# Six buffers for spilled activations, expert rows three ahead, the first eight tiles' gates kept in SBUF, and stores on ScalarE's queue

## The chip, the cores and the metric

The kernel runs on one core of a Trainium2 chip. The metric is device time in microseconds (us) of one execution. Engines are called as the profile calls them: PE is TensorE's matrix multiply and PEld its weight load, DVE is VectorE, ACT is ScalarE, POOL is GpSimd, SP is SyncE, which issues most DMAs. SPq, POOLq and so on are the engines' queues of DMA issues and waits.

## The reference, cut to what matters

One decoder layer on 512 prompt tokens and 64 sample tokens: a gated short convolution and a sliding-window attention are merged, a layer norm follows, and then a mixer that picks experts by product keys. The mixer is where the change lies:

```python
def block_fn(xb):                       # tokens x 1024, 8 heads, 128 x 128 experts
    qv = jnp.einsum('nd,de->ne', xb, w_pq).reshape(PEER_BLOCK, PEER_HEADS, 2, D_HALF)
    s = jnp.einsum('nhpc,hpkc->nhpk', qv, sub_keys)
    top_s, top_i = lax.top_k(s, PEER_TOPK)                      # 16 of 128, per half
    cand_s = top_s[:, :, 0, :, None] + top_s[:, :, 1, None, :]
    best_s, sel = lax.top_k(cand_s.reshape(PEER_BLOCK, PEER_HEADS, -1), PEER_TOPK)
    ...
    gate = jax.nn.softmax(best_s, axis=-1)
    pre = jnp.einsum('nd,nhkd->nhk', xb, expert_u[idx])
    coef = gate * jax.nn.gelu(pre, approximate=False)
    return jnp.einsum('nhk,nhkd->nd', coef, expert_v[idx])
```

A second layer norm closes the layer.

## The kernel before, in words

Every product runs in three passes (`mm3`): each operand is split into a high part `whi` (copied by ACT, L119) and a remainder `wlo` (subtracted by POOL or DVE, L120). `table` loads a 512 KB weight block into `raw` (SP's queue, L138), splits it, and then lets `side` run some steps of side work.

The tokens are split in two. For 192 rows (`GATHER`) the chosen experts' rows are fetched one by one: `experts` issues one gather per step on POOL's queue (L512, 128 rows of 4 KB, 512 KB), and DVE folds a fetched row into a dot product (`junk`, L526) or into the output (`h`, L535). There are 384 such steps, and the tables `PACE_A`, `PACE_B`, `PACE_U` and `PACE_V` say how many are taken beside each weight block. The other 384 rows (`DENSE`) go through all 16384 experts, 128 at a time, in 128 tiles t:

- `front(t)`: 24 matmuls of 384 columns (L123 to L125) and a gelu on ACT. The first `NS` tiles are stored to DRAM (`spill`), the next `LAG` stay in SBUF (`gel`); so 69 fronts run ahead of the closing loop.
- `gate_matrix`: 24 groups of 16 tokens. DVE builds one-hot matrices (`hot`, L787, four per group), ACT and POOL scale them by the gates, PE multiplies them (L796), ACT and DVE copy the product to `gb`, and SP stores it to the DRAM tensor `gd` (L803). A scheduler that simulates the engines weaves the first 59 fronts around the scores and the groups; the ten fronts 59 to 68 are held behind the last group.
- the closing loop: `middle(t)` loads the gates of eight tiles at a time from `gd` into `gm` (L902) and the stored activation into `re` (L906), and multiplies them (L910); `back(t)` loads a block of `expert_v` (`raw<-in_ev`); 18 matmuls of 512 columns (L940) add the tile to six accumulators. Fronts 69 to 127 run in the second part of the same loop. The last two tiles' matmuls are L134.

`route` picks 16 of the candidates and turns their scores into gates (L447 to L452). `finish` is the closing layer norm (L190, L548 to L554), after which SP stores the output. The order of instructions on each engine is fixed when the kernel is built. Pools share SBUF by region: pool `v`, which holds `re`, `gm` and the `expert_v` blocks of later tiles, takes the place of pools that are closed before it.

Of the kernel before, what the change touches and what calls it, by code (L numbers as in the profile page):

```python
# [47 lines left out]
GN = 16  # L48
# [20 lines left out]
PACE_A, PACE_B, PACE_U, PACE_V = (1, 0), (2, 1, 1), (2, 1), (1, 3)  # L69
# [6 lines left out]
def step_kernel(ctx: ExitStack, tc: tile.TileContext, I: dict, O: dict):  # L76
# [86 lines left out]
    mask_p = const("mask_p", [128, 256], src=I["mask_p"])  # L163
# [9 lines left out]
    kT_all = const("kT_all", [128, SEQ])  # L173
    v_all = const("v_all", [128, 5, 128])
# [233 lines left out]
    def top16(val, pos, s, n):  # L408
        s2 = tmp("k", [128, 128], "s2", bufs=2)[:s.shape[0], :n]
        V.max(val[:, 0:8], s)  # L410
        V.max_index(pos[:, 0:8], val[:, 0:8], s)
        V.match_replace(s2, val[:, 0:8], s, -3.0e38)
        V.max(val[:, 8:16], s2)
        V.max_index(pos[:, 8:16], val[:, 8:16], s2)

    numbers, scratch = [iota], []

    def route(val, pos, sel, hs):

# [13 lines left out]
        def f128(tag, dt=F32):  # L433
# [15 lines left out]
        gs = scratch[0][:r, 128:132] if scratch else tmp("k", [128, 4], "gs")[:r]  # L449
        V.tensor_reduce(gs, ge, axis=AX.X, op=ALU.add)  # L450
        V.reciprocal(gs, gs)
        V.tensor_tensor(gt.rearrange("p (h k) -> p h k", h=4), ge,  # L452
                        gs.unsqueeze(2).broadcast_to([r, 4, 16]), op=ALU.mult)

        mk = f128("mk")
        V.tensor_single_scalar(mk, bp, 64, op=ALU.is_ge)
        pf = tmp("k", [128, 4, 2, 16], "pf", dt=BF16)[:r]
        V.tensor_copy(pf, pos.rearrange("p (h s) k -> p h s k", s=2))
        for k, (s1, s2, off) in enumerate((((4, ALU.logical_shift_right), (2, ALU.logical_shift_right), -12.0),
# [9 lines left out]
            oh = tmp("k", [128, 4, 16, 16], "oh", dt=BF16)[:r]  # L469
# [111 lines left out]
    def weight(s, src):  # L581
# [3 lines left out]
        if s.units > LO_N:  # L585
            return table(src, "w", G)
# [146 lines left out]
    def scores(s, g4):  # L733
# [21 lines left out]
        for i, r in enumerate(s.rows):  # L755
# [3 lines left out]
            sc = tmp("kb"[s.w], [128, 4, 128], "sc", bufs=2 + s.w * 2)  # L759
# [14 lines left out]
    def gate_matrix(i, keys, gt, gd):  # L774
# [6 lines left out]
        for g in range(128 // GN):  # L781
# [21 lines left out]
            S.dma_start(gd[i * (128 // GN) + g], gb)  # L803
# [48 lines left out]
    pools["b"] = bs.enter_context(pool("b", "right"))  # L852
# [3 lines left out]
    def front(t):  # L856
        wu = table(I["euT"][t], "w", G if t < AHEAD else V, PACE_U[t % len(PACE_U)] if t < AHEAD else 0)
# [194 lines left out]
```

## Time and profile before

| what | us |
|---|---|
| median of three runs (lowest, highest) | 1848.39 (1845.89, 1849.37) |
| the profiled execution, whole | 1850.18 |
| its span, first to last instruction | 1848.4 |
| PE busy | 1723.9 (93%) |
| PE weight loads busy | 1566.4 (85%) |
| DVE busy | 1464.7 (79%) |
| ACT busy | 781.4 (42%) |
| POOL busy | 1109.6 (60%) |

PE is busy 93% of the span, but its matmuls overlap and their ends are modelled, so the rate at which they start tells more than the busy time. The 124 us in which PE is idle are not spread evenly, and neither is the work of the DMA engines: the page's slices show 130 GB/s near the start and 300 to 350 GB/s in the second half. Each stage has to be read for itself.

### The profile page before, as it was taken

What the parts mean: (1) busy time and instruction counts of PE and PEld (TensorE: products, weight loads), DVE (VectorE), ACT (ScalarE), POOL (GpSimd) and SP (SyncE); (2) the same over time, 40 slices, a digit from 0 to 9 for tenths busy, and PEclk for the clock granted to TensorE, in tenths of its full rate; (3) what the DMA queues carried; (4) which work ended last, traced back from release to release, by engine and by line L of the source; (5) the groups of instructions that cost most, each with busy time, mean ns of one, the idle gap of its engine ahead of it and who ended that gap; (6) DMA issues with size and microseconds to landing.
All of it is one profiled execution on the core that took longest, in us unless ns stands there. A gap on an engine that the chain in (4) does not pass through costs nothing.

```text
span 1848.4 us, 27569 instructions
## 1 busy us (share of the span) xinstructions
PE 1723.9 (93%) x9760; PEld 1566.4 (85%) x9760; DVE 1464.7 (79%) x2588; ACT 781.4 (42%) x1337; POOL 1109.6 (60%) x724
## 2 busy tenths in 40 slices
PE   7999998998799999899888899999999999999985
PEld 7998898988489899799878778778999999999974
DVE  5634579998965699987893778779788878888887
ACT  4554444443233344377794333333333333343322
POOL 4445434367857777798645422224678787778783
PEclk9999999999989999899999999999999999999998
DMA  7446443368757789899748899999999999989873
GB/s 252 134 150 225 138 132 122 115 200 300 249 201 241 235 294 311 271 349 348 289 188 303 317 333 335 336 346 339 333 314 345 337 324 350 353 307 343 314 268 104
DMA packets 190539, 496.50 MB, mean 269 GB/s; under 512 B 17712, under 2 KB 83696, under 8 KB 187312
## 3 DMA queue, kind: packets, MB, share of 16 engines
q1 hardware_dynamic: 135104, 293.39, 46.5%
q0 software_dynamic: 55296, 201.35, 30.2%
q8 instruction: 76, 1.25, 0.3%
q14 instruction: 63, 0.52, 0.1%
HBM read 454.48 MB, written 40.54 MB: 268 GB/s over the span
## 4 chain that ended last, share of the span: by engine, by line
PE 40%; DVE 23%; DMA 14%; issue 9%; POOL 8%; ACT 4%; SPq 1%; DVEq 0%; POOLq 0%; ACTq 0%
PE acc L940 15%; PE ps L123 7%; PE ps L124 7%; PE ps L125 7%; DMA g<-in_ev,idx 5%; POOL wlo L120 4%; POOL g L512 4%; DVE junk L526 3%; PE ps L796 3%; DMA re<-spill 2%; DVE wlo L120 2%; DMA raw<-in_ev 2%; DMA raw<-in_w_o 1%; ACT whi L119 1%; ACT hot L793 1%
## 5 line engine op out<-in xcount | busy, mean ns | idle before, releaser
L120 POOL TENSOR_TENSOR wlo<-raw,whi 128x1024 fp32r<-128x1024 f32 x232 | 579.1, 2499 | 301.8 <-ACT whi L119 264.7
L119 ACT ACTIVATE whi<-raw 128x1024 fp32r<-128x1024 f32 x388 | 409.5, 1056 | 603.9 <-PE ps L124 236.1
L123 PE MATMUL ps<-xhi,whi 128*128 128x384 f32 (+2 forms) x1600 | 529.9, 331 | 21.6 <-ACT sp L863 13.4
L125 PE MATMUL ps<-xhi,wlo 128*128 128x384 f32 (+2 forms) x1600 | 526.1, 329 | 3.5 <-POOL wlo L120 2.0
L124 PE MATMUL ps<-xlo,whi 128*128 128x384 f32 (+2 forms) x1600 | 526.1, 329 | 0.0
L535 DVE SCALAR_TENSOR_TENSOR h<-g,pre,h 128x1024 f32<-128x1024 f32 x192 | 309.8, 1614 | 68.3 <-DMA g<-in_ev,idx 66.8
L512 POOL DMA_INDIRECT g<-in_eu,idx x192 | 204.2, 1063 | 233.1 <-DVE junk L526 186.9
L123 PEld LDWEIGHTS ps<-xhi,whi 128*128 128x128 f32 x1600 | 308.4, 193 | 31.0 <-ACT sp L863 15.1
L512 POOL DMA_INDIRECT g<-in_ev,idx x192 | 257.0, 1338 | 124.9 <-DVE h L535 77.9
L125 PEld LDWEIGHTS ps<-xhi,wlo 128*128 128x128 f32 x1600 | 307.8, 192 | 5.3 <-POOL wlo L120 2.3
L124 PEld LDWEIGHTS ps<-xlo,whi 128*128 128x128 f32 x1600 | 308.3, 193 | 2.9 <-issue 0.3
L940 PE MATMUL acc<-whi,chi 128*128 128x512 f32 x756 | 291.4, 392 | 14.5 <-ACT chi L119 8.2
L940 PE MATMUL acc<-wlo,chi 128*128 128x512 f32 x756 | 296.9, 393 | 7.6 <-POOL wlo L120 7.6
L940 PE MATMUL acc<-whi,clo 128*128 128x512 f32 x756 | 256.4, 392 | 1.1 <-DVE clo L120 1.1
L120 DVE TENSOR_TENSOR wlo<-raw,whi 128x1024 fp32r<-128x1024 f32 x156 | 203.5, 1304 | 46.0 <-ACT whi L119 43.6
L940 PEld LDWEIGHTS acc<-whi,chi 128*128 128x128 f32 x756 | 142.6, 189 | 46.7 <-ACT chi L119 11.5
L940 PEld LDWEIGHTS acc<-wlo,chi 128*128 128x128 f32 x756 | 142.4, 188 | 38.0 <-POOL wlo L120 9.7
L526 DVE SCALAR_TENSOR_TENSOR junk<-g,hp 128x1024 bf16<-128x1024 f32 x104 | 125.9, 1210 | 56.8 <-DMA g<-in_eu,idx 54.8
L940 PEld LDWEIGHTS acc<-whi,clo 128*128 128x128 f32 x756 | 142.4, 188 | 31.3 <-DVE clo L120 1.6
L526 DVE SCALAR_TENSOR_TENSOR junk<-g,h 128x1024 bf16<-128x1024 f32 x88 | 130.9, 1488 | 3.3 <-DMA g<-in_eu,idx 3.0
L796 PE MATMUL ps<-hot 128*128 128x128 f32 x768 | 113.4, 290 | 14.5 <-ACT hot L793 13.4
L787 DVE TENSOR_TENSOR hot<-pt,T 128x1024 f32<-128x1024 f32 x96 | 113.9, 1218 | 15.8 <-PE ps L796 12.7
(250 smaller groups left out, 2157.9 us busy)
## 6 DMA issues: line engine op xcount, KB each, us to landing
raw<-in_euT SPq DMA_DIRECT2D x128, 512.0 KB
raw<-in_ev SPq DMA_DIRECT2D x128, 512.0 KB
gd<-gb SPq DMA_DIRECT2D x24, 1024.0 KB
gm<-gd SPq DMA_DIRECT2D x48, 512.0 KB
raw<-in_w_g SPq DMA_DIRECT2D x32, 512.0 KB
raw<-in_w_pq SPq DMA_DIRECT2D x32, 512.0 KB
raw<-in_w_bch SPq DMA_DIRECT2D x24, 512.0 KB
spill<-sp SPq DMA_DIRECT2D x60, 192.0 KB
```

The costliest lines, as they stand in the source:

```text
L119: A.activation(hi, src, AF.Copy)
L120: return (eng or V).tensor_tensor(lo, src, hi.bitcast(F32), op=ALU.subtract)
L123: PE.matmul(ps, L[0], R[0], start=start, stop=False)
L124: PE.matmul(ps, L[0], R[1], start=False, stop=False)
L125: PE.matmul(ps, L[1], R[0], start=False, stop=stop)
L512: G.indirect_dma_start(out=rows[i], out_offset=None, in_=I[src], in_offset=bass.IndirectOffsetOnAxis(ap=idx[c][:, s:s + 1], axis=0))
L526: V.scalar_tensor_tensor(junk, g, 1.0, in_psum(c), op0=ALU.mult, op1=ALU.mult, accum_out=p)
L535: V.scalar_tensor_tensor(h_tok[c], g, p, h_tok[c], op0=ALU.mult, op1=ALU.add)
L787: V.tensor_tensor(hot, iota_ps.unsqueeze(1).unsqueeze(1).broadcast_to([128, 2, 4, 128]), T[:, 0:2, n:n + 4].unsqueeze(3).broadcast_to([128 ...
L793: A.activation(oi, oi, AF.Copy, scale=weight_of)
L796: newest[1] = PE.matmul(ps[:, r * 128:(r + 1) * 128], hot[:, 1, r, :], oi, start=True, stop=True).ins
L940: PE.matmul(*args, **kw)
```

## The change

The constants: `NS` 60 to 63 and `LAG` 9 to 6 (three more tiles are spilled, still 69 fronts ahead), `GBUF` 4 to 5 and `GLAG` 2 to 3 (five row buffers, gathers issued three steps ahead), `OB` 3 to 4 (one-hot buffers). `re` gets six buffers for three. Each group's gates are stored in two pieces: tiles 8 and on to `gd`, the first eight straight into the SBUF tile `gm` by a 64 KB copy. The stores to `spill` are issued by ACT instead of SP. The side steps are paced anew: one beside each of the second half's 16 `w_pq` blocks, three beside each front from 59 on, two in three tiles (before, one per tile) while the closing loop reads spilled tiles, and three per tile afterwards as before. The gates' softmax is taken out of `route` and done once per chunk of rows by a new function. Buffers move between pools (`q`, `kv`, `f2`) to make room.

```diff
-NS = 60
-LAG = 9
+NS = 63
+LAG = 6
...
-GBUF = 4
-GLAG = 2
+GBUF = 5
+GLAG = 3
...
-OB = 3
+OB = 4
...
-PACE_A, PACE_B, PACE_U, PACE_V = (1, 0), (2, 1, 1), (2, 1), (1, 3)
+PACE_A, PACE_B, PACE_Q, PACE_U, PACE_V = (1, 0), (2, 1, 1), 1, (2, 1), (1, 3)
...
+    def softmax16(x, nh):
+
+        r = x.shape[0]
+        x3 = x.rearrange("p (h k) -> p h k", h=nh)
+        gs = tmp("k", [128, 8], "gs")[:r, :nh]
+        A.activation(gs, x3[:, :, 0], AF.Copy)
+        V.tensor_tensor(x3, x3, gs.unsqueeze(2).broadcast_to([r, nh, 16]), op=ALU.subtract)
+        A.activation(x, x, AF.Exp)
+        V.tensor_reduce(gs, x3, axis=AX.X, op=ALU.add)
+        V.reciprocal(gs, gs)
+        V.tensor_tensor(x3, x3, gs.unsqueeze(2).broadcast_to([r, nh, 16]), op=ALU.mult)
...
-        b3 = bv.rearrange("p (h k) -> p h k", h=4)
-        ge = f128("ge").rearrange("p (h k) -> p h k", h=4)
-        V.tensor_tensor(ge, b3, b3[:, :, 0:1].broadcast_to([r, 4, 16]), op=ALU.subtract)
-        A.activation(ge, ge, AF.Exp)
...
         if s.units > LO_N:
-            return table(src, "w", G)
+            return table(src, "w", G, PACE_Q)
...
                 route(s.val[i], s.pos[i], s.sel[i], g4 // 2)
+                if g4 == 3:
+                    softmax16(s.sel[i][1], 8)
...
-            S.dma_start(gd[i * (128 // GN) + g], gb)
+            at = i * (128 // GN) + g
+            S.dma_start(gd[at, :, IB:, :], gb[:, IB:, :])
+            S.dma_start(head[:, at], gb[:, :IB, :])
...
-    pools["b"] = bs.enter_context(pool("b", "right"))
+    pools["f2"] = ctx.enter_context(pool("f2", "right"))
+    gm = {0: tmp("f2", [128, NG, IB, GN], "gm")}
+    pools["b"] = bs.enter_context(pool("b0", "right"))
...
-        wu = table(I["euT"][t], "w", G if t < AHEAD else V, PACE_U[t % len(PACE_U)] if t < AHEAD else 0)
+        wu = table(I["euT"][t], "w", G if t < AHEAD else V, (PACE_U[t % len(PACE_U)] if t < AHEAD - KEEP else 3) if t < AHEAD else 0)
...
-            S.dma_start(spill[t], ge)
+            A.dma_start(spill[t], ge)
...
-        if t % IB == 0:
-            gm[0] = tmp("v", [128, NG, IB, GN], "gm", bufs=2)
+        if t % IB == 0 and t:
+            gm[0] = tmp("f2" if t // IB % 2 == 0 else "v", [128, NG, IB, GN], "gm")
...
-            ge = tmp("v", [128, ND], "re", bufs=3)
+            ge = tmp("v", [128, ND], "re", bufs=6)
...
-                   PACE_V[t >= NS])
+                   PACE_V[1] if t >= NS else PACE_V[0] * (t % 3 > 0))
```

The built order shows what that moves. On SP's queue, where the one-hot groups end and the closing loop begins, there stood before (`gd<-gb` stores a group's gates, `gm<-gd` loads those of eight tiles, `re` a spilled tile, `raw` a weight block of the fronts, `in_euT`, or of the accumulations, `in_ev`):

```order
L803 DMA gd<-gb 128x2048 x13
L902 DMA gm<-gd 128x8x128
L864 DMA spill<-sp 128x384
L902 DMA gm<-gd 128x8x128 x2
L906 DMA re<-spill 128x384 x2
L138 DMA raw<-in_euT 128x1024
L906 DMA re<-spill 128x384
L902 DMA gm<-gd 128x8x128 x3
L138 DMA raw<-in_ev 128x1024 x3
L138 DMA raw<-in_euT 128x1024
L906 DMA re<-spill 128x384 x2
L138 DMA raw<-in_euT 128x1024
```

And in the changed kernel, from the last group's two stores on:

```order
L807 DMA gd<-gb 128x1920
L808 DMA gm<-gb 128x128
L922 DMA re<-spill 128x384 x5
L138 DMA raw<-in_euT 128x1024
L922 DMA re<-spill 128x384
L918 DMA gm<-gd 128x8x128
L922 DMA re<-spill 128x384
L918 DMA gm<-gd 128x8x128 x2
L922 DMA re<-spill 128x384
L138 DMA raw<-in_ev 128x1024 x3
L138 DMA raw<-in_euT 128x1024 x2
L138 DMA raw<-in_ev 128x1024
```

The stores to `spill` are gone from this queue; one set of three `gm` loads stands ahead of the first `expert_v` block and of the last two front blocks, where before there were two sets.

On POOL, around the second half's scores (the four `w_pq` blocks of a score group and the fronts beside them), there stood before:

```order
L512 DMA g<-in_eu,idx_95 128x1024
L120 TENSOR_TENSOR wlo<-raw,whi 128x1024
L512 DMA g<-in_eu,idx_95 128x1024 x2
L120 TENSOR_TENSOR wlo<-raw,whi 128x1024 x5
L512 DMA g<-in_eu,idx_95 128x1024
L120 TENSOR_TENSOR wlo<-raw,whi 128x1024
L512 DMA g<-in_eu,idx_95 128x1024 x2
```

And now:

```order
L511 DMA g<-in_eu,idx_92 128x1024
L120 TENSOR_TENSOR wlo<-raw,whi 128x1024
L511 DMA g<-in_eu,idx_92 128x1024 x2
L120 TENSOR_TENSOR wlo<-raw,whi 128x1024
L511 DMA g<-in_eu,idx_92 128x1024
L120 TENSOR_TENSOR wlo<-raw,whi 128x1024
L511 DMA g<-in_eu,idx_92 128x1024
```

Five blocks in a row had no gather between them; now each block has one.

At the end of POOL's order, the last gathers and the last blocks of `expert_v` (tiles 119 to 124) stood before as:

```order
L120 TENSOR_TENSOR wlo<-raw,whi 128x1024
L512 DMA g<-in_ev,idx_98 128x1024 x3
L120 TENSOR_TENSOR wlo<-raw,whi 128x1024
L512 DMA g<-in_ev,idx_98 128x1024 x3
L120 TENSOR_TENSOR wlo<-raw,whi 128x1024
L512 DMA g<-in_ev,idx_98 128x1024
L120 TENSOR_TENSOR wlo<-raw,whi 128x1024
L512 DMA g<-in_ev,idx_98 128x1024 x3
L120 TENSOR_TENSOR wlo<-raw,whi 128x1024 x2
```

And now, for tiles 119 to 124 as well:

```order
L120 TENSOR_TENSOR wlo<-raw,whi 128x1024
L511 DMA g<-in_ev,idx_95 128x1024 x3
L120 TENSOR_TENSOR wlo<-raw,whi 128x1024
L511 DMA g<-in_ev,idx_95 128x1024 x2
L120 TENSOR_TENSOR wlo<-raw,whi 128x1024 x4
```

The last four blocks have no gather between or behind them; before, the last two.

## Rows read from the trace of the kernel before

**Rows 1.** Windows: us; PE, PEld, DVE, ACT, POOL busy (instructions); clock; DMA share, GB/s.

```profile
640.00:800.00 160.00, 145.10 (x823) 142.35 (x824) 159.55 (x447) 70.01 (x111) 124.82 (x83) 0.95 0.84 285
800.00:880.00 80.00, 80.00 (x547) 80.00 (x547) 63.94 (x80) 57.91 (x142) 70.26 (x66) 1.00 0.97 361
909.00:978.50 69.50, 56.76 (x380) 50.84 (x380) 63.76 (x65) 62.69 (x181) 28.38 (x47) 0.95 0.47 192
978.50:1033.30 54.80, 44.62 (x243) 43.87 (x242) 22.53 (x25) 17.60 (x24) 30.34 (x18) 0.92 0.89 305
...
1076.00:1280.00 204.00, 195.95 (x857) 160.01 (x856) 163.36 (x246) 72.69 (x97) 48.76 (x48) 1.00 0.98 336
1300.00:1740.00 440.00, 440.00 (x2227) 400.59 (x2226) 372.29 (x322) 159.59 (x219) 341.48 (x208) 1.00 0.93 332
1777.50:1831.00 53.50, 43.48 (x181) 32.90 (x179) 43.30 (x45) 13.58 (x20) 30.83 (x18) 1.00 0.55 182
1831.00:1848.40 17.40, 0.04 (x1) 0.00 (x0) 12.86 (x22) 4.93 (x8) 6.19 (x4) 0.58 0.24 91
```

**Rows 2.** Waits, 978.5 to 1033.3 us: total us, times, longest us.

```profile
ACT whi L119 <- DMA raw<-in_ev: 11.2, 3, 10.0
```

**Rows 3.** The chain that ended last, 976 to 1013 us: start us, us, what.

```profile
994.61 5.43 SPq L902
...
1000.08 2.97 SPq L138
...
1003.10 8.19 DMA raw<-in_ev
```

**Rows 4.** Timeline of PE in the held-back fronts: start us, us, what.

```profile
979.10 0.34 PE L123 MATMUL ps<-xhi,whi 128*128 128x384 f32 x1
...
991.58 0.33 PE L123 MATMUL ps<-xhi,whi 128*128 128x384 f32 x1
```

**Rows 5.** Waits in the accumulations, 1076 to 1280 us.

```profile
DVE re L910 <- DMA re<-spill: 27.2, 10, 4.4
...
ACT chi L119 <- DVE re L910: 11.3, 13, 3.3
```

**Rows 6.** Waits in the tail, 1777.5 to 1831 us.

```profile
PE acc L940 <- POOL wlo L120: 7.6, 5, 2.9
```

**Rows 7.** POOL's groups by line, 1777.5 to 1831 us: busy us, mean ns, idle before.

```profile
L512 POOL DMA_INDIRECT g<-in_ev,idx x12 | 16.1, 1340 | 3.7 <-issue 2.1 <-DVE h L535 1.3 <-DMA g<-in_ev,idx 0.2
L120 POOL TENSOR_TENSOR wlo<-raw,whi 128x1024 fp32r<-128x1024 f32 x6 | 15.1, 2529 | 1.7 <-ACT whi L119 1.7
```

**Rows 8.** Timeline of DVE: its first sum of a dense chunk.

```profile
1827.08 1.27 DVE L947 SCALAR_TENSOR_TENSOR h<-h,acc 128x512 f32<-128x512 f32 x2
```

**Rows 9.** Timeline of PE: first and last of the closing 30 matmuls.

```profile
1823.94 0.39 PE L134 MATMUL acc<-whi,chi 128*128 128x512 f32 x1
...
1830.65 0.39 PE L134 MATMUL acc<-whi,sp 128*128 128x512 f32 x1
```

**Rows 10.** Waits in the scores of the second half, 640 to 800 us.

```profile
ACT ge L448 <- DVE ge L447: 19.5, 4, 7.8
...
PE ps L123 <- ACT sp L863: 12.9, 3, 6.3
...
POOL g L512 <- DVE junk L526: 7.5, 6, 2.9
```

**Rows 11.** DVE's groups by line, 600 to 800 us.

```profile
L526 DVE SCALAR_TENSOR_TENSOR junk<-g,hp 128x1024 bf16<-128x1024 f32 x50 | 60.3, 1206 | 17.0 <-DMA g<-in_eu,idx 16.8
...
L447 DVE TENSOR_TENSOR ge<-bv 128x64 f32<-128x64 f32 x5 | 4.7, 949 | 0.0
```

**Rows 12.** Timeline of DVE in the one-hot groups.

```profile
958.38 4.81 DVE L787 TENSOR_TENSOR hot<-pt,T 128x1024 f32<-128x1024 f32 x4
...
963.71 4.81 DVE L787 TENSOR_TENSOR hot<-pt,T 128x1024 f32<-128x1024 f32 x4
```

**Rows 13.** The spill stores on SP: issue ns, least, median, most; first and last start.

```profile
L864 SPq DMA_DIRECT2D spill<-sp x60: 319/327/1787, 542.3 to 985.1; - x60
```

More of the change, by code (lines that the diff above doesn't have):

```diff
@@ L408, in top16 @@
     def top16(val, pos, s, n):
-        s2 = tmp("k", [128, 128], "s2", bufs=2)[:s.shape[0], :n]
+        s2 = tmp("q", [128, 128], "s2", bufs=2)[:s.shape[0], :n]
         V.max(val[:, 0:8], s)
@@ L416, in step_kernel @@
     numbers, scratch = [iota], []
+    def softmax16(x, nh):
[8 more added lines that the diff above has]
+        V.tensor_tensor(x3, x3, gs.unsqueeze(2).broadcast_to([r, nh, 16]), op=ALU.mult)
     def route(val, pos, sel, hs):
-        keys, gt = sel
+        keys, best = sel
         r = val.shape[0]
         val, pos = (t[:, hs * 8:hs * 8 + 8, :] for t in (val, pos))
-        gt, keys = gt[:r, hs * 64:hs * 64 + 64], [t[:r, hs * 64:hs * 64 + 64] for t in keys]
-        cand = tmp("k", [128, 4, NCAND], "cand")[:r]
+        keys = [t[:r, hs * 64:hs * 64 + 64] for t in keys]
+        cand = tmp("q", [128, 4, NCAND], "cand")[:r]
         v4 = val.rearrange("p (h s) k -> p h s k", s=2)
@@ L437, in f128 @@
                 return t if dt == F32 else t.bitcast(dt)
-            return tmp("k", [128, 64], tag, dt=dt)[:r]
-        bv = f128("bv")
+            return tmp("q", [128, 64], tag, dt=dt)[:r]
         bp = f128("bp", U32)
+        bv = best[:r, hs * 64:hs * 64 + 64]
         for h in range(4):
             top16(bv[:, h * 16:(h + 1) * 16], bp[:, h * 16:(h + 1) * 16], cand[:, h, :], NCAND)
-        b3 = bv.rearrange("p (h k) -> p h k", h=4)
-        ge = f128("ge").rearrange("p (h k) -> p h k", h=4)
-        V.tensor_tensor(ge, b3, b3[:, :, 0:1].broadcast_to([r, 4, 16]), op=ALU.subtract)
-        A.activation(ge, ge, AF.Exp)
[L449 to L453, printed above, removed]
         mk = f128("mk")
         V.tensor_single_scalar(mk, bp, 64, op=ALU.is_ge)
-        pf = tmp("k", [128, 4, 2, 16], "pf", dt=BF16)[:r]
+        pf = tmp("q", [128, 4, 2, 16], "pf", dt=BF16)[:r]
         V.tensor_copy(pf, pos.rearrange("p (h s) k -> p h s k", s=2))
@@ L764, in scores @@
                 keys, gt = s.sel[i]
-                kh, gh = [tmp("k", [128, 64], f"kh{k}") for k in range(2)], tmp("k", [128, 64], "gh")
+                kh, gh = [tmp("q", [128, 64], f"kh{k}") for k in range(2)], tmp("q", [128, 64], "gh")
                 route(s.val[i], s.pos[i], (kh, gh), 0)
+                softmax16(gh, 4)
                 for dst, src in zip((*keys, gt), (*kh, gh)):
@@ L811, in step_kernel @@
     pools["k"] = ks.enter_context(pool("k", "left"))
+    qs = ExitStack()
+    pools["q"] = qs.enter_context(pool("q", "left"))
     pools["mm"] = ks.enter_context(psum("mm", 3))
+    kvs = ExitStack()
+    pools["kv"] = kvs.enter_context(pool("kv", "right"))
+    mask_p, kT_all = tmp("kv", [128, 256], "mask_p"), tmp("kv", [128, SEQ], "kT_all")
+    v_all = tmp("kv", [128, 5, 128], "v_all")
+    loads.insert(0, (mask_p, I["mask_p"]))
     at_stack = ExitStack()
@@ L843, in step_kernel @@
         late(ln2[k], I["ln"][2 + k].broadcast_to([128, D]))
+    kvs.close()
     at_stack.close()
@@ L880, in step_kernel @@
         fronts(FQ * (k + 1))
+    qs.close()
+    bs.close()
+    pools["b"] = bs.enter_context(pool("b", "right"))
     total = len(DENSE) * 128 // GN
@@ L883, in step_kernel @@
     for i in range(len(DENSE)):
-        for g in gate_matrix(i, *second.sel[i], gd):
+        for g in gate_matrix(i, *second.sel[i], gd, gm[0]):
             fronts(base + (AHEAD - KEEP - base) * (i * (128 // GN) + g + 1) // total)
```

12 lines of the change are left out of this document (4 added, 8 removed).

## The prediction

> **What bounds the kernel now.** I read the windows by stage first, since a busy share over the whole span hides which stage waits. PE sets the pace in most of them: in the long mixed part of the closing loop it is busy for all 440 us [rows 1]. What a stage can give back is the time in which PE could have started matmuls and did not, so I need PE's own rate. In the held-back fronts 24 groups of three matmuls start in 991.58 - 979.10 = 12.48 us [rows 4], 0.173 us each, so a front (24) takes 4.16 us. In the mixed part 2227 matmuls take 440 us [rows 1]; 42 of them, a front and an accumulation, take 8.30 us, which leaves 4.14 us for the accumulation. The closing 30 matmuls start 6.71 us apart, first to last [rows 9]; 18 of those take 4.16 us. I use 4.15 us for an accumulation.
>
> Against that, four places lose time. (1) From the last one-hot group to the first accumulation 54.8 us pass [rows 1], and PE has ten fronts to do, 41.6 us: 13.2 us are lost. The waits name ACT standing 10.0 us for a block of `expert_v` [rows 2], and the chain says why it is late: SP is held for 5.43 us at one load of the second set of `gm`, then three blocks are issued, and the first takes 8.19 us to land [rows 3]. ACT works in order, so the blocks and gelus of the last fronts wait behind it. The gates are needed only later; it is their queue place that costs. (2) The accumulations that read spilled tiles: 857 matmuls in 204 us [rows 1], 4.285 us per tile, 0.135 over PE's rate, with the DMA engines busy 98% at 336 GB/s. DVE waits 27.2 us for `re`, and ACT 11.3 us behind DVE [rows 5]. (3) The tail after the last front: ten accumulations take 53.5 us [rows 1] and would take 41.5. PE waits for POOL's `wlo` [rows 6], and POOL alternates 1.34 us gathers with 2.53 us subtractions [rows 7]: three gathers and one subtraction are 6.6 us per tile, against 4.15 on PE. (4) The scores of the second half: DVE is busy 159.55 of 160 us and PE only 145.10 [rows 1]; ACT waits for DVE at the gates' softmax and PE waits for ACT behind it [rows 10].
>
> **Term A, the step into the closing loop.** The first eight tiles' gates need no trip through DRAM, and six `re` buffers let the first loads go at once. In the new SP order one set of `gm` loads stands ahead of the `expert_v` blocks and of the last two front blocks, not two. The set that held SP is gone from there, but the bytes are not few. Between the last group's store and the second accumulation's block, SP and ACT move eight `re` (1536 KB), six `gm` loads (3072), three `euT` (1536), seven `ev` blocks (3584), four spill stores (768) and the last gate store (960), 11456 KB; with some eleven gathers of 512 KB, since three now go beside each of these fronts, it is 17088 KB or 17.5 MB. At 336 GB/s [rows 1] that is 52.1 us, and PE has ten fronts and one accumulation, 45.75 us, to cover it. So 6.4 us of the 13.2 stay lost: A = -6.8. Bounds: 0, if DMA is as late as before, and -13.2. Here a rule can be set against the row. The Trainium skill, "SBUF — State Buffer", section "A bandwidth-pool intuition that's wrong (but worth ruling out)", puts HBM to one core at about 358 GB/s. By that figure the 17.5 MB take 48.9 us, an estimate, and A would be -10.0; this trace's stretch of 204 us at 98% share moved 336, so the sum goes by 336.
>
> **Term B, accumulations from spilled tiles.** Steps of side work are cut from one to two in three tiles. In the changed order DVE folds 48 rows between the first block and the 60th, against 62 before: 0.24 of 512 KB less per tile, 0.126 MB. Now 336 GB/s for 4.285 us is 1.44 MB per tile; 1.31 MB take 3.91 us, below PE's 4.15. The `re` waits go with it. Three more spilled tiles only move accumulations here from the tail. 62 tiles can win 0.135 each, 8.4 us; I take B = -6, as 94% DMA load leaves some lateness. Bounds 0 and -8.4.
>
> **Term C, the tail.** The changed POOL order ends its gathers with tile 121's block, so the seven accumulations behind the last front have none beside them and POOL needs 2.5 us per tile. Of 12.0 lost us I take 11 back. The one left is for the sample rows' closing norm, which now stands on DVE and ACT ahead of the last splits; three accumulations' worth of time covers it. Bounds -5 and -12.
>
> **Term D, the end.** From PE's last matmul 17.4 us pass [rows 1]. DVE starts the first dense chunk at 1827.08 [rows 8], when PE had finished that chunk 24 matmuls before its end, at 1831 - 5.6 = 1825.4; the sample rows' norm stood in the way. D = -2, bounds 0 and -4.
>
> **Term E, one-hot buffers.** Alone, a group takes 963.71 - 958.38 = 5.33 us, filled by DVE's four `hot` (4.81) and a copy [rows 12]. A fourth buffer does not shorten DVE's work; in the new order twelve groups stand alone instead of thirteen. E = -1, bounds 0 and -3.
>
> **Term F, rows brought forward.** 115 rows are folded before the first one-hot, 92 before. Each is 1.206 us on DVE [rows 11], 23 rows 27.7 us. Nine of them come before DVE is full; the other fourteen, 16.9 us, land where it has 0.45 us free in 160. Two softmaxes of five go, at least their 0.949 us subtraction each, 1.9 us [rows 11]: 15.0 us remain. Two more fronts now stand ahead of the first one-hot, 8.3 us in which PE needs no DVE. F = +7, bounds +15 (no cover; DVE idles 16 of 80 us right after, so it does not spread further [rows 1]) and -5 (fewer softmax stops; they cost PE part of 12.9 us [rows 10]).
>
> **At no cost.** The spill stores take SP 0.327 us each [rows 13]; on ACT 63 of them are 20.6 us, beside fronts, where ACT is busy 57.91 of 80 us at most [rows 1]. If ACT were last there, that is the price. The 24 copies into `gm` take as long on SP, which waits for the groups anyway. Three more stored tiles add 1.2 MB, 3.5 us of DMA at 336 GB/s, inside B's slack. Five row buffers and three ahead leave the same number of rows, two, between a gather and the fold that frees its buffer, so POOL waits as before and DVE less for landings. Other pools' new places in the first 600 us I cost at nothing: they move some instructions, but no wait that I can name.
>
> **Sum.** -6.8 - 6 - 11 - 2 - 1 + 7 = -19.8. The profiled execution took 1850.18 us, so it would be 1830.4; it stands 1.8 over the median of the runs, 1848.39, and on that footing I forecast 1829. All bounds on one side give -45.6 and +10.0: 1803 and 1858.
>
> **Rivals.** *POOL stands behind the rows* (slower). In the second half's scores each block's subtraction now has a gather ahead of it on POOL, and a gather waits for DVE's fold two rows back, in a stage where DVE is full. If each of 16 waits as long as the longest now, 2.9 us [rows 10], PE's blocks come 46.4 us late; the rest of the sum gives -26.8, so it ends at 1868. It decides from 26.8 / 16 = 1.7 us per row. For it: DVE has no slack. Against it: the six waits there now total 7.5 us, 1.25 each [rows 10]. Chance 0.09.
>
> *DMA keeps the transition and the accumulations* (A and B nothing; the change then does not do there what it says, since `expert_v` blocks and not gates hold PE). The gathers brought forward go into the stretch that is fullest, three per front; 1848.4 - 11 - 2 - 1 + 7 = 1841. For it: 98% share [rows 1]; against it: 14 rows less in the stage. Chance 0.20.
>
> *The tail keeps its gathers* (C nothing): if rows slip behind in the mixed part, where POOL is busy 341 of 440 us and DVE 372 [rows 1], the last ones again fall behind the last front: 1840. Against it, PE loses nothing there at the same three rows per tile. Chance 0.08.
>
> *Everything is given back and F is covered*: A -13.2, B -8.4, C -12, D -4, E -1: 1810. Chance 0.13.
>
> **How the numbers follow.** The forecast, 1820 to 1838, holds 0.50. Only the first rival ends above the kernel before. Faster by over 0.2% (3.7 us, about what a measurement of this kernel can tell from no change) has 0.86, within it 0.04, slower 0.10. The range 1806 to 1845 leaves out the first rival and the outer edge of the others.
>
> **What the profile would show.** A: the step from the last one-hot to the first accumulation near 48 us, ACT no longer waiting 10 us for `in_ev`; wrong if it stays above 53 or DMA share is 1.0 with PE idle. B: 4.15 to 4.2 us per tile in the accumulations and no long wait for `re`. C: seven accumulations after the last front in about 29 us, no wait of PE for POOL's `wlo`. D: 15 us or so after PE's last matmul. F: PE idle in the scores 15 to 25 us; 40 or more, with POOL waiting for DVE's folds, is the first rival. The forecast is wrong above all if DVE's lateness in the scores reaches PE uncovered, or if gathers and blocks together outrun the DMA engines.

## The result: slower by 1.2%

The changed kernel takes 1868.63 us in the median of four runs (1862.01 to 1879.36), the kernel before beside it 1848.56: a ratio of 1.0117, 95% interval 1.0068 to 1.0165. The forecast was 1829. Run once more on another chip it gave 1.0126 (1.0093 to 1.0159). The profiled execution took 1868.24 us, its span is 1866.5.

The windows of the changed kernel, cut at front 16, front 44, inside the one-hot groups, at the last group, the first accumulation, the first front of the mixed part, the last front and the last matmul (columns as in [rows 1]):

```profile
666.60:809.50 142.90, 126.15 (x691) 124.20 (x691) 137.34 (x394) 56.43 (x88) 110.45 (x73) 0.94 0.88 302
809.50:909.00 99.50, 99.50 (x694) 99.49 (x693) 84.40 (x103) 78.41 (x197) 86.22 (x84) 1.00 0.94 339
909.00:987.50 78.50, 64.93 (x430) 59.02 (x429) 74.91 (x84) 66.00 (x190) 39.69 (x58) 0.93 0.64 249
987.50:1053.40 65.90, 43.86 (x241) 42.58 (x239) 33.80 (x45) 17.55 (x24) 39.34 (x27) 0.86 0.98 349
1053.40:1331.30 277.90, 264.13 (x1116) 211.73 (x1117) 183.03 (x255) 91.45 (x123) 45.90 (x44) 0.98 0.84 276
1331.30:1821.50 490.20, 490.20 (x2480) 446.32 (x2480) 450.47 (x363) 176.72 (x241) 371.01 (x228) 1.00 0.92 328
1821.50:1852.40 30.90, 29.46 (x127) 23.25 (x125) 18.59 (x32) 11.65 (x17) 5.06 (x2) 1.00 0.09 26
1852.40:1866.50 14.10, 0.03 (x1) 0.00 (x0) 8.48 (x16) 3.70 (x7) 5.73 (x4) 0.58 0.30 112
```

The windows of the kernel before at three of the same cuts (front 16, front 44, last group; spilled tiles):

```profile
662.60:805.20 142.60, 130.09 (x742) 128.45 (x741) 140.76 (x374) 64.97 (x107) 113.64 (x78) 0.95 0.88 300
805.20:978.70 173.50, 159.05 (x1072) 151.81 (x1071) 147.58 (x167) 137.85 (x364) 117.12 (x131) 0.98 0.76 289
...
1033.30:1282.70 249.40, 241.35 (x1045) 197.32 (x1046) 198.13 (x299) 86.39 (x114) 67.03 (x62) 0.99 0.97 338
```

Stage by stage, with 4.15 us of PE per accumulation:

| stage | before, us | after, us | change | forecast |
|---|---|---|---|---|
| start to front 16 | 662.6 | 666.6 | +4.0 | 0 |
| front 16 to the last one-hot group (E, F) | 142.6 + 173.5 | 142.9 + 99.5 + 78.5 | +4.8 | +6 |
| the step (A) | 54.8 | 65.9 | +11.1 | -6.8 |
| spilled tiles, beyond 4.15 each (B) | 249.4 for 58: 8.7 | 277.9 for 62: 20.6 | +11.9 | -6 |
| tail, beyond 4.15 each (C) | 53.5 for 10: 12.0 | 30.9 for 7: 1.9 | -10.1 | -11 |
| after the last matmul (D) | 17.4 | 14.1 | -3.3 | -2 |

The rows add up to +18.4; the mixed part, with 59 accumulations for 60 (490.2 us for 494.8), gives 0.4 back beyond 4.15 each, and the spans differ by 18.1. The +4.0 of the first row tells nothing: in the profiles below of kernels that have this stretch as the changed kernel has it, it takes some 661 to 674 us. C and D came as forecast. The loss is in A and B, the two places that the change's buffers were to help.

In the step the DMA engines are full: 98% at 349 GB/s, 23.0 MB in 65.9 us, where the kernel before moved 16.7 MB (54.8 us at 305 GB/s [rows 1]). The chain of the step goes through landings (start us, us, what):

```profile
997.47 12.97 DMA re<-spill
...
1011.12 9.91 DMA raw<-in_ev
...
1036.27 8.02 DMA raw<-in_ev
```

POOL's groups in the step, changed kernel:

```profile
L511 POOL DMA_INDIRECT g<-in_eu,idx x19 | 20.2, 1063 | 11.3 <-DVE junk L525 9.1 <-issue 1.7 <-DMA re<-spill 0.3
```

Nineteen gathers of 512 KB lie in this stretch, for ten in the kernel before; the forecast counted eleven.

In the spilled tiles it is the opposite: the DMA engines are less busy than before (84% for 97%, 276 GB/s for 338), yet each tile takes 4.48 us. The waits there (us in total, times, longest):

```profile
DVE re L926 <- DMA re<-spill: 78.1, 39, 6.6
PEld acc L956 <- DVE clo L120: 22.0, 21, 4.4
```

DVE's wait for `re` was 27.2 us [rows 5] with three buffers, and is 78.1 with six. A timeline of SP and DVE shows why (L926 is the product of a stored tile with its gates; L120 `clo` is the remainder of that product, which PE needs; SP's rows are the issue and the wait for it):

```profile
1193.48 0.56 DVE L926 TENSOR_TENSOR re<-re,gm 128x384 f32<-128x384 f32 x1 [2.98 <-DMA re<-spill]
1193.96 0.55 DVE L120 TENSOR_TENSOR clo<-re,chi 128x384 fp32r<-128x384 f32 x1
1194.43 1.22 DVE L120 TENSOR_TENSOR wlo<-raw,whi 128x1024 fp32r<-128x1024 f32 x1
1194.54 0.32 SPq L922 DMA_DIRECT2D re<-spill  x1
...
1197.24 0.56 DVE L926 TENSOR_TENSOR re<-re,gm 128x384 f32<-128x384 f32 x1 [0.45 <-DVE junk L525]
1197.72 0.55 DVE L120 TENSOR_TENSOR clo<-re,chi 128x384 fp32r<-128x384 f32 x1
...
1198.30 0.32 SPq L922 DMA_DIRECT2D re<-spill  x1
...
1202.47 0.56 DVE L926 TENSOR_TENSOR re<-re,gm 128x384 f32<-128x384 f32 x1 [1.92 <-DMA re<-spill]
1202.95 0.55 DVE L120 TENSOR_TENSOR clo<-re,chi 128x384 fp32r<-128x384 f32 x1
```

A tile's last use of its `re` buffer is the subtraction `clo`. SP issues the load of the tile six ahead a moment after it (1194.54 after 1193.96), and the next product in DVE's order (1197.24) is the product of just that load; that of the load issued at 1198.30 stands at 1202.47, after 1.92 us of waiting. The next `clo`, on which PE waits, stands behind that product. So a full landing lies between two tiles' `clo`, whatever the number of buffers. Counted in DVE's built order, six products stand ahead of the `clo` of tile 30 that are not yet split, all six buffers; before, it was two of three, and a load had one more tile's time to land. In the kernel before, at the same place, the product of the load issued at 1190.81 is the one at 1198.43, 7.6 us later, and another tile's product (1194.09) stands between; DVE waits 0.18 us.

```profile
1190.23 0.55 DVE L120 TENSOR_TENSOR clo<-re,chi 128x384 fp32r<-128x384 f32 x1
1190.70 0.55 DVE L910 TENSOR_TENSOR re<-re,gm 128x384 f32<-128x384 f32 x1
1190.81 0.33 SPq L906 DMA_DIRECT2D re<-spill  x1
...
1194.09 0.55 DVE L910 TENSOR_TENSOR re<-re,gm 128x384 f32<-128x384 f32 x1
...
1198.43 0.56 DVE L910 TENSOR_TENSOR re<-re,gm 128x384 f32<-128x384 f32 x1 [0.18 <-DMA re<-spill]
```

### The profile page after: what moved, and what is told of

It reads as the page before. It is cut to its first block, busy times and chain, and to the rows that moved or that the text cites. A ratio compares the mean times of both kernels' runs of the same rounds, so it can differ in the third digit from the quotient of the medians.

```text
span 1866.5 us, 27644 instructions
## 1 busy us (share of the span) xinstructions
PE 1732.5 (93%) x9760; PEld 1569.4 (84%) x9760; DVE 1476.6 (79%) x2575; ACT 775.8 (42%) x1336; POOL 1087.8 (58%) x721
## 4 chain that ended last, share of the span: by engine, by line
PE 26%; DMA 11%; issue 5%; DVE 4%; ACT 2%; POOL 2%; SPq 0%; DVEq 0%; POOLq 0%; ACTq 0%
PE acc L956 15%; DMA re<-spill 7%; PE ps L125 4%; PE ps L123 4%; PE ps L124 4%; ACT hot L796 1%; DMA g<-in_ev,idx 1%; DVE wlo L120 1%; DVE clo L120 1%; POOL g L511 1%; DMA raw<-in_ev 1%; POOL wlo L120 1%; ACT gb L803 1%; DMA gm<-gd 1%; DMA gm<-gb 0%
## 5 line engine op out<-in xcount | busy, mean ns | idle before, releaser
L120 POOL TENSOR_TENSOR wlo<-raw,whi 128x1024 fp32r<-128x1024 f32 x229 | 576.2, 2518 | 347.2 <-ACT whi L119 317.5
L123 PE MATMUL ps<-xhi,whi 128*128 128x384 f32 (+2 forms) x1600 | 529.2, 331 | 25.9 <-ACT sp L878 16.8
L511 POOL DMA_INDIRECT g<-in_ev,idx x192 | 238.2, 1240 | 174.8 <-DVE h L534 106.8
L534 DVE SCALAR_TENSOR_TENSOR h<-g,pre,h 128x1024 f32<-128x1024 f32 x192 | 295.3, 1538 | 35.5 <-DMA g<-in_ev,idx 33.5
L956 PE MATMUL acc<-whi,clo 128*128 128x512 f32 x756 | 279.3, 397 | 13.7 <-DVE clo L120 13.4
L120 DVE TENSOR_TENSOR wlo<-raw,whi 128x1024 fp32r<-128x1024 f32 x159 | 206.0, 1296 | 37.6 <-ACT whi L119 37.4
L525 DVE SCALAR_TENSOR_TENSOR junk<-g,hp 128x1024 bf16<-128x1024 f32 x135 | 163.4, 1211 | 46.7 <-DMA g<-in_eu,idx 44.2
L799 PE MATMUL ps<-hot 128*128 128x128 f32 x768 | 111.4, 292 | 13.6 <-ACT gb L803 7.4
L790 DVE TENSOR_TENSOR hot<-pt,T 128x1024 f32<-128x1024 f32 x96 | 112.5, 1214 | 13.9 <-PE ps L799 5.6
L799 PEld LDWEIGHTS ps<-hot 128*128 128x128 f32 x768 | 104.5, 199 | 19.4 <-ACT hot L796 10.4
```

Of the source, the lines that this page charges most:

```text
L120: return (eng or V).tensor_tensor(lo, src, hi.bitcast(F32), op=ALU.subtract)
L123: PE.matmul(ps, L[0], R[0], start=start, stop=False)
L511: G.indirect_dma_start(out=rows[i], out_offset=None, in_=I[src], in_offset=bass.IndirectOffsetOnAxis(ap=idx[c][:, s:s + 1], axis=0))
L525: V.scalar_tensor_tensor(junk, g, 1.0, in_psum(c), op0=ALU.mult, op1=ALU.mult, accum_out=p)
L534: V.scalar_tensor_tensor(h_tok[c], g, p, h_tok[c], op0=ALU.mult, op1=ALU.add)
L790: V.tensor_tensor(hot, iota_ps.unsqueeze(1).unsqueeze(1).broadcast_to([128, 2, 4, 128]), T[:, 0:2, n:n + 4].unsqueeze(3).broadcast_to([128 ...
```

## The experiments

Two theories came out of this. **Order**: in the spilled tiles the product stands too early in DVE's order (rival: bandwidth, the loads are late since DMA is shared). **Bytes**: three rows beside each held-back front fill the DMA engines in the step (rivals: queue, what stands ahead of the `expert_v` blocks; and folds, DVE's or POOL's own time). Ratios are to the kernel before on the same chip, with their 95% intervals. The kernel before had medians of 1850 to 1855 us there.

**1. Products later, same buffers** (`late4`).

```diff
-        V.tensor_tensor(g3, g3, gm[0][:, :, t % IB, :], op=ALU.mult)
+        with tc.issue_after(clo_of[t - 4]) if t >= 4 else ExitStack():
+            V.tensor_tensor(g3, g3, gm[0][:, :, t % IB, :], op=ALU.mult)
...
-        split(co[0], co[1], ge)
+        clo_of[t] = split(co[0], co[1], ge).ins
```

> The changed kernel, all six buffers kept, but on DVE the product of tile t with its gates may not stand ahead of the subtraction clo of tile t - 4, so a load has about two tiles' time to land. Order theory (DVE reaches the product of the sixth tile ahead right behind the clo that frees that tile's buffer, and waits there for a load that was issued a moment before): accumulations from spilled tiles fall from 4.48 to 4.15 to 4.2 us each, 17 to 20 us less, about 1850, and DVE's wait for re falls from 78 us to under 15. Bandwidth theory (the loads are late since the DMA engines are shared with blocks and rows): still 4.4 or more, 1865 or more. The step from the last one-hot group to the first accumulation stays near 66 us by both.

Measured: 0.9943 (0.9914 to 0.9971). The windows (step, spilled tiles):

```profile
987.60:1054.60 67.00, 44.93 (x240) 43.67 (x239) 31.29 (x43) 17.22 (x24) 38.96 (x27) 0.84 0.91 322
1054.60:1310.20 255.60, 255.58 (x1117) 211.43 (x1118) 187.37 (x258) 91.56 (x124) 47.47 (x46) 0.99 0.93 311
```

DVE's wait in the second of these, then the timeline, where the product now stands behind a later `clo` and finds its data there (the product at 1192.85 is that of a load issued at 1184.81):

```profile
DVE re L929 <- DMA re<-spill: 13.6, 7, 2.4
```

```profile
1188.30 0.56 DVE L120 TENSOR_TENSOR clo<-re,chi 128x384 fp32r<-128x384 f32 x1 [0.76 <-ACT chi L119]
1188.77 0.55 DVE L929 TENSOR_TENSOR re<-re,gm 128x384 f32<-128x384 f32 x1
1188.88 0.32 SPq L924 DMA_DIRECT2D re<-spill  x1
...
1192.38 0.56 DVE L120 TENSOR_TENSOR clo<-re,chi 128x384 fp32r<-128x384 f32 x1 [0.76 <-ACT chi L119]
1192.85 0.55 DVE L929 TENSOR_TENSOR re<-re,gm 128x384 f32<-128x384 f32 x1
```

62 tiles in 255.6 us are 4.12 each: PE's own rate, 22.3 us gained by one edge in the order, and at a higher DMA rate (311 GB/s for 276). DVE's wait for `re` falls from 78.1 to 13.6 us. The profiled spans differ by 22.0 us, as this stage does; the ratios differ by 1.7%, some 32 us, with intervals wide enough for both. The order theory holds, bandwidth falls as the cause of the loss; the step stays, as both said.

**2. The old pace of the held-back fronts** (`hold21`).

```diff
-... (PACE_U[t % len(PACE_U)] if t < AHEAD - KEEP else 3) if t < AHEAD else 0)
+... PACE_U[t % len(PACE_U)] if t < AHEAD else 0)
```

> The changed kernel with the ten held-back fronts paced as before (two and one steps in turn, not three). Bytes theory (17 gathers of 512 KB in the step, 9 before, fill the DMA engines): eight gathers or so fewer, 4.2 MB, 12 us at 349 GB/s: the step from the last one-hot group to the first accumulation falls from 65.9 us to 54 to 58. Queue theory (what stands ahead of the expert_v blocks on SP and ACT makes them late): it stays at 63 or more. By both the gathers end four tiles later, so the seven closing accumulations lose up to 8 us again: 1862 to 1867 by the first, 1870 or more by the second.

Measured: 0.9934 (0.9906 to 0.9962). The windows (front 44 to the last group, the step, the first 40 spilled tiles, the next 18, what follows the last matmul):

```profile
803.70:975.90 172.20, 163.32 (x1123) 157.00 (x1122) 152.71 (x175) 144.53 (x386) 119.82 (x136) 0.98 0.79 292
...
975.90:1024.00 48.10, 44.31 (x240) 43.95 (x239) 19.17 (x24) 13.89 (x20) 30.26 (x18) 0.93 0.96 333
...
1024.00:1189.60 165.60, 163.93 (x721) 134.91 (x721) 118.12 (x172) 62.10 (x83) 28.55 (x30) 1.00 0.92 312
1189.60:1274.50 84.90, 77.92 (x325) 62.05 (x324) 55.81 (x86) 26.95 (x37) 11.24 (x12) 0.96 0.83 267
1812.30:1837.60 25.30, 0.01 (x1) 0.00 (x0) 20.55 (x37) 6.82 (x12) 6.76 (x4) 0.57 0.26 83
```

POOL's gathers in the step:

```profile
L511 POOL DMA_INDIRECT g<-in_eu,idx x10 | 10.6, 1063 | 2.1 <-issue 1.5 <-DVE junk L525 0.3 <-DMA raw<-in_euT 0.2
```

The step falls by 17.8 us to 48.1, more than expected: POOL issues 10 gathers in it, not 19, and a shorter step also moves fewer blocks, 16.0 MB in all. It is not the place in the queue: SP issues the first `expert_v` block 22.3 us into this step and 23.6 us into that of the changed kernel. The stretch ahead of it is 5.8 us shorter. The tail did not grow, but the rows left over end behind the last matmul, 25.3 us for 14.1. The spilled tiles also gained, which nobody expected: the other pace gave another built order. Mostly four or five products stand ahead there up to tile 30, mostly six or more from tile 40 on; and 40 tiles take 4.14 us each, the next 18 take 4.72. That fits the order theory again, inside one kernel. So the time, 1841.45 us, is 20 us or more under what either theory expected.

**3. Bytes or folds.** Three kernels change only what 38 rows of these fronts do, and leave DVE's order of products nearly as in the changed kernel (five or six ahead). `half` fetches half rows, `nofold` fetches all but folds 8 of 1024 elements, `nogather` folds a resident row and fetches none; their outputs are others for it.

```diff
half      +  G.indirect_dma_start(out=rows[i][:, :512], in_=I[src].rearrange("r (a d) -> (r a) d", a=2), ...)
nofold    +  V.scalar_tensor_tensor(junk[:, :8], g[:, :8], 1.0, in_psum(c)[:, :8], ...)
nogather  +  rows[i] = h_tok[c]; return
```

> The changed kernel, but the gathers of 38 rows (the 149th to the 186th, those of the held-back fronts and of the step) fetch half rows, 256 KB for 512, other data than the reference's, and DVE's fold reads that half twice, so that its time and POOL's issue stay. Bytes theory: 17 x 0.262 = 4.5 MB less in the step, 18.9 MB, at 350 GB/s 54 us for 65.9; about 1856. Engine theory (POOL's issues and DVE's folds between the blocks' subtractions make the step long, not the bytes): 64 us or more, 1866 or more.

> The changed kernel with all its gathers, but the folds of the same 38 rows read 8 of 1024 elements, so DVE has 1.1 us less to do for each and frees the row's buffer sooner; the output is another. Gathers theory: the step stays at 62 us or more, or grows, as the gathers go out sooner. Folds theory: it falls to 56 or less. From front 44 to the last one-hot group: 173 to 175 us by the folds theory, 179 or more by the gathers theory. Spilled tiles 4.4 us or more.

> The changed kernel without the gathers of 38 rows (the 149th to the 186th, those of the held-back fronts and of the step); DVE folds a resident row in their place, so its time stays and the output is another. If it is the gathers that make the step long, by their bytes or by POOL's issues, it falls from 66 us to 42 to 48 (PE needs 41.6). If DVE's folds do, it stays at 55 or more. In the stretch from front 44 to the last one-hot group the folds theory (six more folds beside lone groups, 1.2 us each) expects 179 to 181 us as in the changed kernel, the gathers theory 173 to 175. Spilled tiles stay at 4.4 us or more, since DVE's order is as it was.

Measured: 1.0034 (0.9999 to 1.0068), 1.0064 (1.0041 to 1.0088) and 0.9953 (0.9923 to 0.9983). The step in `half`:

```profile
977.40:1035.00 57.60, 42.50 (x241) 41.22 (x240) 33.67 (x46) 17.59 (x24) 40.04 (x27) 0.92 0.96 329
```

In `nofold`:

```profile
984.50:1049.50 65.00, 45.61 (x241) 44.37 (x239) 15.90 (x45) 17.44 (x24) 38.10 (x27) 0.89 0.99 351
```

In `nogather`:

```profile
1005.80:1053.50 47.70, 43.46 (x241) 42.82 (x240) 16.51 (x20) 15.78 (x22) 19.31 (x8) 0.96 0.85 282
```

Without the folds DVE works 15.9 us for 33.8 and the step stays at 65.0 us: folds fall as a cause. Without the gathers it is 47.7, and the DMA engines are no longer full. With half the bytes it is 57.6, about halfway, with the same 19 issues on POOL; expected was 54, at 350 GB/s, but half rows moved at 329. So with 19 gathers in it the step is in the main bytes over the rate of the DMA engines. Not all of it need be: in `late4` and in `b_pace3`, below, it is as long at a DMA share of 91%.

What the runs don't settle is the stretch ahead of the step, 5.8 us longer with three rows per front. DVE has 35 folds there in the changed kernel, 29 in `hold21`, and 50 in `nogather`, where 18 folds of the resident row come between the one-hot matrices: the stretch takes 178.0, 172.2 and 192.5 us, about 1 us more for each fold of 1.21 us. That speaks for the folds, but no run shows it alone: `nofold` (177.8 us) and `half` (178.2 us) changed only three of the 35 rows folded in this stretch, so they don't test it. Spilled tiles stayed slow in all three: in `nogather` 4.37 us a tile, a little under what was expected, with DMA only 77% busy.

**4. The pace alone, in the kernel before** (`b_pace3`): the `hold21` edit the other way round, and nothing else.

> The kernel before, with nothing changed but three steps beside each held-back front. Bytes theory: some six more gathers, 3.1 MB, in the step, and the blocks and gates that go with a longer one: 54.6 us becomes 58 to 64. The gathers end some five tiles earlier, so the ten closing accumulations fall from 53.5 to 42 to 45 us. Both together 1838 to 1848 on a chip where the kernel before takes 1848. Engine theory: the step stays at 55 and the time falls to 1834 to 1839.

Measured: 1.0102 (1.0058 to 1.0147). Front 44 to the last group, step, spilled tiles, tail, end:

```profile
817.80:996.30 178.50, 159.85 (x1072) 152.18 (x1071) 153.96 (x179) 138.03 (x364) 123.45 (x137) 0.97 0.80 300
996.30:1066.20 69.90, 45.64 (x241) 44.38 (x240) 30.62 (x44) 17.48 (x24) 39.75 (x27) 0.84 0.91 318
1066.20:1313.50 247.30, 241.50 (x1045) 197.28 (x1045) 195.52 (x280) 85.86 (x114) 63.46 (x61) 0.99 0.98 338
1811.50:1858.40 46.90, 43.30 (x181) 34.02 (x179) 22.72 (x37) 17.63 (x25) 14.83 (x6) 0.96 0.19 60
1858.40:1872.40 14.00, 0.00 (x0) 0.00 (x0) 8.41 (x15) 3.62 (x7) 5.74 (x4) 0.69 0.30 112
```

With this one number the kernel before measures as slow as the changed one, over the expected 1838 to 1848; its stages explain half of that. The step takes 69.9 us, over the expected 58 to 64, with 19 gathers in it for 10, where six more were expected. The stretch ahead of it takes again 5.0 more, with 35 folds for 29; the tail and the end give back 10.0. The stages from front 44 on sum to some +11 us, the medians say +20. Of the profile's own +24, 12.6 come before front 44 (at 817.8, before at 805.2), where the engines' orders are still the same; why the median has the rest stays open.

**5. Both edits together, and a row per spilled tile as before the change** (`late4_hold21`; `late4_hold21_v1` with `PACE_V[0]` for `PACE_V[0] * (t % 3 > 0)`).

> Both edits together: products no more than four tiles ahead of clo, held-back fronts at two and one steps. If order and bytes are the two causes, the gains add: 1868 - 18 - 10 + up to 8 for the tail's gathers, 1842 to 1850. If one of them is not a cause, it stays at 1855 or more.

> As the one with both edits, and one step beside every spilled tile's accumulation as before the change, not beside two in three, so that the gathers end early again. Order theory: with the products late enough the accumulations carry one row per tile at 4.15 to 4.25 us, as DMA needs 1.44 MB per tile and 336 to 349 GB/s give it in 4.1 to 4.3; the tail keeps its 31 us: 1836 to 1842. Bandwidth theory: the accumulations go back to 4.3 or more and it ends at 1848 or more.

Measured: 0.9871 (0.9832 to 0.9911), 1831.37 us; and 0.9850 (0.9812 to 0.9887), 1826.25 us, both some 10 us under what was expected. Step and spilled tiles of the first, then the spilled tiles of the second:

```profile
984.20:1029.40 45.20, 43.30 (x241) 42.98 (x240) 18.58 (x24) 14.94 (x21) 30.82 (x18) 0.96 0.92 332
1029.40:1284.10 254.70, 253.37 (x1119) 209.53 (x1118) 186.82 (x274) 93.82 (x127) 46.97 (x46) 1.00 0.94 318
...
1026.30:1301.20 274.90, 263.08 (x1144) 215.06 (x1143) 209.08 (x295) 96.90 (x129) 76.81 (x65) 0.99 0.96 332
```

Both gains stand in one kernel, stage by stage. The ratios don't simply add: alone the two edits bring the changed kernel's time down by 1.7 and 1.8%, together by 2.4%, in part since the pace alone had already put some of the order right (266.8 us for the spilled tiles, for 277.9). With two rows in three tiles the spilled tiles take 4.10 us and the end 23.6; with a row per tile 4.33 us at 96% DMA share and 332 GB/s, and the end 14.0. So in this pair, with the order mended, the accumulations' bytes do count: this is the size that term B was about, and the expected 4.15 to 4.25 was too good.

**6. Undoing single parts**, from `late4_hold21_v1` (the "best so far" of the expectations): no steps beside `w_pq`, spill stores on SP, the first gates through DRAM, three `re` buffers.

```diff
v1_q0      -PACE_Q 1                            +PACE_Q 0
v1_sp      -A.dma_start(spill[t], ge)           +S.dma_start(spill[t], ge)
v1_nohead  -if t % IB == 0 and t:               +if t % IB == 0:   (and one store of all tiles to gd)
v1_re3     -"re", bufs=6, clo_of[t - 4]         +"re", bufs=3, clo_of[t - 2]
```

> The best kernel so far (products at most four tiles ahead, old pace of the held-back fronts, one step per spilled tile) without the steps beside the second half's w_pq blocks. If those rows cost PE time where DVE is full, as forecast (+7 us), the stretch from front 16 to front 44, less 3.6 us for each one-hot group in it, falls from 141 us to 134 to 137; the gathers then end some five tiles later, so the end loses up to 12 us: 1826 to 1835. Rival: the rows there are free, the stretch keeps its time, and only the end loses: 1832 to 1840.

> The best kernel so far with the stores to spill issued on SP again. No-cost theory (as forecast: 63 issues of 0.33 us beside fronts on either engine): the same time within 3 us, 1823 to 1830. Rival: on SP the stores, which wait for a gelu, hold the blocks queued behind them, so the fronts or the step get longer: 1832 or more.

> The best kernel so far, but the first eight tiles' gates go through DRAM: one store of 1024 KB per group, and three loads of gm for the first eight tiles ahead of the first expert_v blocks. Bytes theory: 1.6 MB more in the step, of 16.5: at 350 GB/s 47.4 + 4.5 = 52 us, 1829 to 1832. Queue theory (SP held at that load makes the blocks late, as in the kernel before): 54 us or more, 1833 to 1837.

> The best kernel so far with three re buffers in place of six, and products at most two tiles ahead of clo, so that a load still has a tile's time. If six buffers add nothing once the order is right, it stays at 1823 to 1832, with 4.25 to 4.35 us per spilled tile and a step of 46 to 50 us. If the first six loads going at once are what shortened the step (54.6 to 47.4 us), the step returns to 52 to 55 and the time to 1831 to 1836.

Measured: 0.9892 (0.9843 to 0.9942), 0.9894 (0.9862 to 0.9925), 0.9899 (0.9850 to 0.9947), 0.9845 (0.9798 to 0.9892). None differs from 0.9850 beyond the intervals. Without the head in SBUF the step is 45.4 us, not 52 or 54: neither theory of that run holds, and the short cut for the first gates is worth nothing there. With three buffers the step is 47.8 us and a spilled tile takes 4.18 (1140 matmuls in 264.7 us):

```profile
969.60:1017.40 47.80, 44.21 (x241) 43.89 (x240) 19.20 (x23) 14.72 (x21) 30.68 (x19) 0.93 0.91 325
1017.40:1282.10 264.70, 260.04 (x1140) 213.31 (x1140) 207.48 (x294) 96.01 (x128) 88.91 (x64) 1.00 0.98 340
```

So six buffers give nothing that three do not give with the right order. Without the rows beside `w_pq` front 16 to the last group takes 144.3 + 166.7 us, inside the 308.6 to 318.8 of its sister kernels: no cost of those rows can be told, and the tail and the end lose 37.4 + 19.3 for 28.8 + 14.0.

**7. Rows spread more evenly** (`even`: two in three spilled tiles, four in every fourth later tile; `best`: the same with three buffers), and the changed kernel once more.

> Products at most four tiles ahead of clo, held-back fronts at two and one steps, two steps in three spilled tiles, and beside the later tiles four steps in every fourth tile, three in the others, so that fewer rows are left for the end. If DVE and the DMA engines have the room that the mixed part shows (PE lost nothing there), spilled tiles take 4.11 us, the mixed part keeps 8.3 us per tile, and the end after the last matmul falls from 23.6 to 14 to 18 us: 1815 to 1824. Rival: the rows are late anyway and the end stays long: 1828 to 1834.

> Three re buffers with products at most two tiles ahead of clo, held-back fronts at two and one steps, two steps in three spilled tiles, four in every fourth later tile and three in the others. Spilled tiles 4.1 to 4.15 us, step 47 us, and 3 to 4 us of the tail and the end given back against one step per spilled tile: 1812 to 1820, the same as or a little under the version with three buffers and one step per tile.

> The changed kernel once more, beside the others on one chip: 0.5 to 1.7% over the kernel before; the step at 63 to 69 us and 4.42 to 4.55 us per spilled tile, if these two are the cause of the loss in every execution and not of one.

Measured: 0.9851 (0.9793 to 0.9908), 0.9901 (0.9864 to 0.9939), 1.0126. `even` comes out as forecast, at 1821.73 us. Its spilled tiles take 254.7 us, 4.10 each, but the tail is 36.7 and the end 17.3: most of what it gains over a row per tile it gives back there. `best` misses its forecast, at 1833.59 us. Its spilled tiles take 4.18 us with two rows in three tiles, as `v1_re3`'s do with a row per tile, though its DMA engines are 90% busy for 98%. Two of its three products stand ahead of `clo` on most tiles, one in `v1_re3`, which may be why; no run separates the two. So what fewer bytes are worth is shown with six buffers only. The changed kernel again shows a step of 66.4 us, and 285.9 us for 62 spilled tiles, 4.61 each, a little over what was expected. Three versions (`late4_hold21_v1`, `v1_re3`, `even`) are 1.5% under the kernel before and 2.6% under the changed one (0.985 over 1.0117), and can't be told apart; `v1_re3`, 1819.94 us, has the fewest buffers.

## Why the prediction was wrong, step by step

**Term A failed at its count of bytes.** The term took "some eleven gathers"; there were 19, with the blocks of a longer step, 23.0 MB for the 17.5 of the sum, and the step took 65.9 us for the 48 forecast. Three steps beside each of ten fronts are 30 rows, and the count should have been made in POOL's order between the last group and the first accumulation. That the DMA engines would set it was right, and the prediction names the way it could fail, "if gathers and blocks together outrun the DMA engines". `hold21`, which has about the gathers that were counted, took 48.1; that this meets the 48 so closely is in part luck, for `nogather`, with no gathers there and 13.5 MB for 16.0, took 47.7. A second step was wrong too: the set of `gm` loads that held SP was to be gone, but SP issued the first `expert_v` block 23.6 us into the step, for 21.6 before. In `v1_re3` it goes out after 11.0 us, and that step, 47.8 us, is no shorter than the 48.1 of `hold21`: the block's place in the queue is not what costs here. The rate was too low rather than too high: 349 GB/s here, 351 in `nofold`, and 336 in the sum. The Trainium skill, "SBUF — State Buffer", section "A bandwidth-pool intuition that's wrong (but worth ruling out)", gives about 358 GB/s from HBM to a core; these two steps come within 2 to 3% of it, and 80 us of the kernel before moved 361 [rows 1].

**Term B failed at "the `re` waits go with it".** Bytes per tile fell as said, and DMA had room, but the wait that grew was not one of bytes: 78.1 us for 27.2, and 4.48 us per tile. Nothing in the prediction asked where in DVE's order the product of a load stands beside the `clo` that frees its buffer. With the order mended the tiles come out at the term's size: 4.12 us in `late4` for a forecast of 4.15 to 4.2.

**Terms C and D** came at -10.1 and -3.3 for -11 and -2. They are real gains, and rows brought forward pay for them: in `v1_q0`, 16 rows later, 13.9 us of them are gone.

**Terms E and F** together gave +4.8 for +6. That is no proof: the second execution of the changed kernel has 138.8 + 178.1 us there, +0.8, and the sister kernels scatter by 10 us. PE idles 16.8 us in the scores, as the forecast's 15 to 25. What E missed is the stretch with the one-hot groups that stand alone, 5 to 6 us longer with three rows per front. Six more folds on DVE lie there; that they are the cause is likely, not shown.

**Spill stores on ACT** cost nothing and bring nothing (`v1_sp`), as forecast. The Trainium skill, "DMA: Bandwidth & Descriptors", section "Issuing engines are not separate DMA queues", says that the issuing engine only saves time on a sequencer, since the transfers share the same engines; `v1_sp` agrees, at 0.9894 for 0.9850, inside the intervals.

**The rivals.** The slower one ended at 1868, the measured time, by another way: POOL did not hold PE up in the scores. The one with DMA keeping the step and the accumulations named the right resource for A alone, at too low a price, since it let the lateness stay and not grow. Lateness that grows in A and B was in no case, so the range missed.

## What to carry to other kernels

More buffers hide a load only if its consumer stands later in the in-order engine than the instruction that frees the buffer, by at least a landing: count in the built order how many consumers stand ahead of the release, and compare it with the buffers. When side work is paced more densely beside a few stages, sum the bytes of the fullest of them from the order, not from the average. Three buffers with the right order did as well as six.

## What was not expected of the hardware

Stretches with the same order on every engine differ between executions: front 44 begins at 805.2 us in the kernel before and at 817.8 in `b_pace3`, with nothing changed ahead of it and the same order of instructions up to 888 us. The kernel before has medians from 1848.56 to 1854.8 us on the chips of these runs, and the intervals of the ratios reach 0.2 to 0.6% to either side, so 0.2% can hardly be told even beside a run on the same chip.
